# A fused decoder block on one core: first weights on ACT's queue, a 32-byte edge tile, projections in groups of six, and other queues at the seams

## The chip, the core and the metric

The kernel runs on one core of a Trainium2 chip. The core has five engines with in-order queues: TensorE (PE) multiplies matrices, VectorE (DVE), ScalarE (ACT) and GpSimd (POOL) do elementwise work, and SyncE (SP) mostly issues DMAs; ACT can issue DMAs too. The metric is the device time of one execution in microseconds; smaller is better. Every big product takes fp32 operands split in two parts (`ah`/`al`, `oh`/`ol`, `fh`/`fl`, `bh`/`bl`: a rounded high part, and the rest), so that one product of 128x128 by 128x512 costs three matmuls: high by high, high by low, low by high.

## What is computed

One decoder block on 1024 positions of 1024 channels, in float32:

```python
xn = rms_norm(x, norm1_g)
proj = xn @ w_in                      # 5632 columns
q_sb, k_sb, v_sb, q_hg, f_hg, i_hg, g_hg, gate_sb, gate_hg = split_cols(proj, IN_SIZES)
o_sb = stick_breaking_attention(rms_norm(heads(q_sb)), rms_norm(heads(k_sb)), heads(v_sb))
o_hg = hgrn2_mixer(q_hg, f_hg, i_hg, g_hg, lb, hg_norm_g)
mixed = sigmoid(gate_sb) * (o_sb @ w_branch[:512]) + sigmoid(gate_hg) * (o_hg @ w_branch[512:])
h = x + mixed @ w_out
hn = rms_norm(h, norm2_g)
out = h + (silu(hn @ w_gate) * (hn @ w_up)) @ w_down      # hidden size 2816
```

## The kernel before

`hybrid_block` is one program of six stages; the positions are handled in two halves of 512 columns (`hs(h)`).

**Start.** SP loads the small vectors (`vt`, L226) and then, in turn, pieces of x (`aa`) and the first four weight halves (`kb`). ACT loads its table at L205. Nine warm-up matmuls on `ones_r` run first. Each piece of x is scaled and split into `ah` (ACT) and `al` (DVE); each weight half into `oh` (POOL) and `ol` (DVE).

**Projections, attention and HGRN** (to about 701 us). All instructions of this stage are collected in a `Plan` and given out at L182 by a list scheduler: it walks a simulated clock and, on each engine, issues the ready instruction that comes first by rank and age. Ring buffers of fixed size (`pj` 3 banks, `z` 2, `ms` 3, `oh` and `ol` 4, `w` 2) hold work back. The projections (`proj`, moving operands `ah`/`al`, output `pj`) have the lowest rank and fill PE between the small products of attention and HGRN (`ms`, `z`). A projection is given out as eight pieces of three matmuls, one for each 128 rows of the contraction. `FILL` sets in which order the projected columns come. Finished heads are stored to `o_d`, gates before the sigmoid to `sig_d`.

**Mixing** (to about 790). SP loads the eight tiles `o_d` into `o32` (L785, ring `ld` of 4); ACT casts them to `oh` (L788), DVE subtracts for `ol` (L789). The branch weights `wb` are loaded through the ring `w` and split through the rings `oh`/`ol` of `wpool`. Gates `s0`, `s1` are loaded (L801, L802), multiplied by the row norm on POOL (L805), put through a sigmoid on ACT (L806), and multiplied into the products (L813, L814).

**wo** (to about 879). For each of eight 128-channel tiles and each half: SP loads a piece of x (`xx`, L856), PE multiplies, DVE adds (L859), SP stores h to `h_d` (L860), DVE scales by the second norm's gain (`yy`, L862), ACT squares and POOL sums the squares in `rr` (L870); DVE and ACT make the operands `fh`/`fl` of the next stage (`make`, L845, L846).

**Gate and up** (to about 1318). 11 rounds `p`, each with two 2x2 Winograd products of seven block products (`winograd`, `prod` at L916): 168 matmuls a round, moving operands `fh`/`fl`. In the first round, `begin` runs `channel_sums` (L924 to L931: the norm's sums over channels). Each round stores its result `c` (L1008) and four combinations `bs` (L1017) to `act_d`, on SP.

**Down** (to the end). Seven block products `o`, each a sum over 11 `p` into four banks `f` (L1060, L1062, L1064), moving operands `bh`/`bl` from `rb`, weights `ah`/`al` from `ra` (L1052, L1053, rings of 6 in `dB`). After the first product SP loads h into `hb` (L1069). After each product DVE adds the four banks to `hb` (L1077), and SP stores finished ones (L1079).

Tiles lie in pools; some are allocated from the right-hand end of a partition (`side="right"`): `rrp`, `qkp`, `const1`, `opool` (with mixing's `oh`, `ol`), `mt`, `s2p`, `fpool` (with `fh`, `fl`). In the program as built, tiles of the right-side pools start at byte addresses that are 32 modulo 64 (`fpool` from 106464, `opool` from 159712), tiles of the others at 0 modulo 64 (`xnp` and `mxp` from 26560, `dB` from 51136).

Of the kernel before, what the change touches and what calls it, by code (L numbers as in the profile page):

```python
# [10 lines left out]
F32 = mybir.dt.float32  # L11
# [4 lines left out]
ALU = mybir.AluOpType  # L16
# [3 lines left out]
P = 128  # L20
S = 1024
D = 1024
KT = D // P
HALF = 512
# [5 lines left out]
FILL = ["GgGGaifq", "gGaGfiqGG", "gaGGGiqGfGG", "gGGG"]  # L30
# [172 lines left out]
def hybrid_block(ctx: ExitStack, tc, xT, wi, wb, wo, wg, wu, wd, vec, outT):  # L203
    nc = tc.nc
    nc.scalar.preload_act_table_set("natural_log_exp_and_others")  # L205

# [19 lines left out]
    nc.sync.dma_start(vt, vec)  # L226
# [17 lines left out]

    rst = ExitStack()
# [47 lines left out]

    def hs(h):
        return slice(h * HALF, (h + 1) * HALF)
# [25 lines left out]
    xn = a_set(xst.enter_context(tc.tile_pool(name="xnp", bufs=1)))  # L321
    pre = ExitStack()
# [22 lines left out]
    st1 = ExitStack()  # L345
# [3 lines left out]
    hgp = st1.enter_context(tc.tile_pool(name="hgp", bufs=1, reuse_waits="tile"))  # L349
# [101 lines left out]
    def take_x(h):  # L451
        ss, acc, ws, sqs = new("ms"), new("tail"), [[], []], []
        for k in range(KT):
            x = new("aa" if h == 0 else ("xf", "xq", "xi", "xg")[k // 2])
            load(x, xT[k][:, hs(h)], 256)
            if h == 0 and k in (0, 1, 3, 4):
                u, i = k % 3, k // 3
                n, v = fill[u]
# [21 lines left out]
    def proj(ws, h, after=None):  # L480

        pss = [new("pj") for _ in ws]
        for k in range(KT):
            cols = slice(k % 4 * P, (k % 4 + 1) * P)
            for ps, w in zip(pss, ws):
                hi, lo = w[k // 4]
                last_fill[0] = M(1536, [
                    (ps, hi[:, cols], xh[k][h][:, hs(h)], k == 0, False),
                    (ps, hi[:, cols], xl[k][h][:, hs(h)], False, False),
                    (ps, lo[:, cols], xh[k][h][:, hs(h)], False, k == KT - 1)],  # L490
                    rank=-1, after=(last_fill[0], after))
            after = None
        return pss
# [67 lines left out]

    COL = {"q": 0, "k": 4, "v": 8, "hq": 12, "hf": 16, "hi": 20, "hg": 24, "G": 28}
# [182 lines left out]
    fill = [("q", 0), ("k", 0), ("v", 0), ("hf", 0), ("hq", 0), ("hi", 0)]  # L745
# [85 lines left out]
    with tc.tile_pool(name="wot", bufs=4, reuse_waits="tile") as ot_:  # L831
        seq = [0, 4, 1, 5, 2, 6, 3, 7]
        wq = [get_w(wo[seq.pop(0)])]
        for i in range(4):
# [14 lines left out]
            for e in range(2):  # L849
# [4 lines left out]
                for h in range(2):  # L854
# [5 lines left out]
                    nc.sync.dma_start(h_d[k][:, hs(h)], xx)  # L860
# [75 lines left out]
    with ExitStack() as sta:  # L936
# [24 lines left out]
        def winograd(a, c, begin=None):  # L961
# [3 lines left out]
            if begin:  # L965
                for ks in ((0, 1, 2), (3,)):
                    for o, bank in ((1, x), (5, z), (6, y)):
                        prod(bank, a[o], fop[o], True, ks)
                begin()
                nc.scalar.copy(p1, x)  # L970
# [8 lines left out]
            prod(x, a[2], fop[2], False)  # L979
# [9 lines left out]
        for p in range(NP):  # L989
# [18 lines left out]
            nc.sync.dma_start(act_d[p][:, :4 * HALF], c.rearrange("p b t -> p (b t)"))  # L1008
# [7 lines left out]
            for b, t in ((4, n7), (5, n6), (6, n5), (7, n4)):  # L1016
                nc.sync.dma_start(act_d[p][:, b * HALF:(b + 1) * HALF], t)  # L1017
# [15 lines left out]
          5: [(d + 4, 1) for d in range(4)], 3: [(d, 1) for d in range(4)]}  # L1033
    bank = [None] * 4
    for o in DOWN:
        first = o in (1, 6, 5)
        for p in range(NP):
            early = o == 1 and p < 4
            wp, tags = bp, btags = dB, ("ah", "al")
            btags = ("bh", "bl")  # L1040
            if early:

                rp = wpool if p < 2 else preB
                raw = rp.tile([P, 1024], F32, tag="w", bufs=2, name="w32")
                ra, rb = raw[:, :512], raw[:, 512:]
                if p < 3:
                    wp = bp = rp
                    tags = btags = ("oh", "ol") if p < 2 else ("ds", "ds")
            else:
                ra = dB.tile([P, HALF], F32, tag="ra", name="ra")  # L1050
                rb = dB.tile([P, HALF], F32, tag="rb", name="rb")
            nc.sync.dma_start(ra, LEFT[o](p))  # L1052
            nc.sync.dma_start(rb, blk(act_d[p], RIGHT[o]))  # L1053
            hi, lo = split(ra, wp, tags)
            bh, bl = split(rb, bp, btags)
            for d in range(4):
                if first and p == 0:
                    bank[d] = fb()
                ws = slice(d * P, (d + 1) * P)
                nc.tensor.matmul(bank[d], hi[:, ws], bh, start=first and p == 0, stop=False,  # L1060
                                 skip_group_check=True)
                nc.tensor.matmul(bank[d], hi[:, ws], bl, start=False, stop=False,  # L1062
                                 skip_group_check=True)
                nc.tensor.matmul(bank[d], lo[:, ws], bh, start=False, stop=p == NP - 1,  # L1064
                                 skip_group_check=True)
        if o == 1:
            for k, h in ([(d, 0) for d in range(4)] + [(d, 1) for d in range(8)]
                         + [(d, 0) for d in range(4, 8)]):
                nc.sync.dma_start(hb[k][:, hs(h)], h_d[k][:, hs(h)])  # L1069
            for d in range(4):  # L1070
                nc.scalar.copy(acc1[d], bank[d])
            continue
        for d, (k, h) in enumerate(TO[o]):
            t = hb[k][:, hs(h)]
            if o in (6, 7, 4):
                nc.vector.tensor_tensor(t, t, acc1[d], op=ALU.add)
            nc.vector.tensor_tensor(t, bank[d], t, op=ALU.add)  # L1077
# [50 lines left out]
```

## Time and profile before

| | us |
|---|---|
| median of 3 runs | 1542.43 (1540.65 to 1542.45) |
| the profiled execution | 1541.46 |
| its span | 1539.7 |
| PE busy | 1515.8 (98%) |
| DVE, ACT, POOL busy | 1184.3, 800.4, 178.8 |

Each page or view is of one profiled execution; times are microseconds from the start of the span. In rows of the timeline the columns are start, duration, engine, line, operation, output<-inputs, count, and in brackets the idle time of that engine just before and what ended it. In rows of groups the columns are line, engine, operation, output<-inputs, shapes, count, then total busy time and mean ns of one, then idle time before. Matmuls overlap in the pipeline, so the time that a matmul costs is the distance from one start to the next, not its own duration. `SPq` and `ACTq` rows are DMA issues on those queues.

The chain that ended last is shared out so: PE 73%, DVE 11%, DMA 6%, ACT 4%, of which `f L916` 25%, `pj L182` 23%, `ms L182` 8%, and `f` of the down stage 12%.

### The profile page before, as it was taken

What the parts mean: (1) busy time and instruction counts of PE and PEld (TensorE: products, weight loads), DVE (VectorE), ACT (ScalarE), POOL (GpSimd) and SP (SyncE); (2) the same over time, 40 slices, a digit from 0 to 9 for tenths busy, and PEclk for the clock granted to TensorE, in tenths of its full rate; (3) what the DMA queues carried; (4) which work ended last, traced back from release to release, by engine and by line L of the source; (5) the groups of instructions that cost most, each with busy time, mean ns of one, the idle gap of its engine ahead of it and who ended that gap; (6) DMA issues with size and microseconds to landing.
All of it is one profiled execution on the core that took longest, in us unless ns stands there. A gap on an engine that the chain in (4) does not pass through costs nothing.

```text
span 1539.7 us, 20478 instructions
## 1 busy us (share of the span) xinstructions
PE 1515.8 (98%) x7213; PEld 1242.1 (81%) x7213; DVE 1184.3 (77%) x2046; ACT 800.4 (52%) x1503; POOL 178.8 (12%) x202
## 2 busy tenths in 40 slices
PE   8999999999999999999999989999999999999999
PEld 6788888888888888888888868778778888778887
DVE  8899679988898768965567798888877777475553
ACT  7866778678768778454333352233333333254442
POOL 4211111111111101114412200000000000000000
PEclk9999999999999999999999999999999999999999
DMA  5111211111111121245334455666633332787672
GB/s 178 41 43 44 76 33 42 59 39 52 50 52 41 59 69 48 71 160 201 125 107 133 139 163 205 217 211 208 213 136 110 105 105 94 270 274 220 193 220 92
DMA packets 78407, 188.53 MB, mean 122 GB/s; under 512 B 9056, under 2 KB 11104, under 8 KB 76896
## 3 DMA queue, kind: packets, MB, share of 16 engines
q1 hardware_dynamic: 73696, 178.83, 35.5%
q10 hardware_dynamic: 4608, 8.39, 1.5%
q8 instruction: 57, 0.93, 0.3%
q14 instruction: 46, 0.38, 0.1%
HBM read 131.61 MB, written 55.57 MB: 122 GB/s over the span
## 4 chain that ended last, share of the span: by engine, by line
PE 73%; DVE 11%; DMA 6%; ACT 4%; issue 4%; POOL 1%; SPq 1%; DVEq 0%; POOLq 0%; ACTq 0%
PE f L916 25%; PE pj L182 23%; PE ms L182 8%; PE f L1062 4%; PE f L1064 4%; PE f L1060 4%; PE z L182 2%; DMA xx<-xT 2%; DVE ol L238 1%; ACT aa L182 1%; DMA rb<-act_d 1%; POOL s L805 1%; DMA s<-sig_d 1%; DVE aa L182 1%; DVE tail L182 1%
## 5 line engine op out<-in xcount | busy, mean ns | idle before, releaser
L182 PE MATMUL pj<-ah,oh 128*128 128x512 f32 x704 | 286.7, 407 | 2.0 <-POOL oh L182 2.0
L182 PE MATMUL pj<-ah,ol 128*128 128x512 f32 x704 | 277.3, 394 | 0.9 <-DVE ol L182 0.9
L182 PE MATMUL pj<-al,oh 128*128 128x512 f32 x704 | 276.0, 392 | 0.0
L916 PE MATMUL f<-fh,oh 128*128 128x512 f32 x616 | 244.0, 396 | 3.4 <-ACT p L970 1.7
L916 PE MATMUL f<-fl,oh 128*128 128x512 f32 x616 | 243.4, 395 | 0.7 <-DVE fl L846 0.7
L916 PE MATMUL f<-fh,ol 128*128 128x512 f32 x616 | 243.2, 395 | 0.6 <-DVE ol L238 0.6
L237 ACT CAST oh<-w 128x512 fp32r<-128x512 f32 x168 | 102.1, 620 | 175.2 <-PE f L916 137.9
L182 PEld LDWEIGHTS pj<-ah,ol 128*128 128x128 f32 x704 | 132.6, 188 | 31.6 <-DVE ol L182 2.1
L182 PEld LDWEIGHTS pj<-ah,oh 128*128 128x128 f32 x704 | 133.1, 189 | 25.3 <-POOL oh L182 2.9
L182 PEld LDWEIGHTS pj<-al,oh 128*128 128x128 f32 x704 | 133.2, 189 | 22.9 <-issue 0.5
L916 PEld LDWEIGHTS f<-fh,oh 128*128 128x128 f32 x616 | 115.4, 187 | 34.3 <-ACT p L970 2.1
L916 PEld LDWEIGHTS f<-fh,ol 128*128 128x128 f32 x616 | 115.4, 187 | 29.1 <-DVE ol L238 1.0
L916 PEld LDWEIGHTS f<-fl,oh 128*128 128x128 f32 x616 | 115.5, 187 | 29.0 <-DVE fl L846 1.0
L238 DVE TENSOR_TENSOR ol<-w,oh 128x512 fp32r<-128x512 f32 x168 | 114.7, 690 | 30.0 <-ACT oh L237 29.8
L1062 PE MATMUL f<-bl,ah 128*128 128x512 f32 x296 | 117.0, 395 | 1.3 <-DVE bl L238 1.3
L1060 PE MATMUL f<-bh,ah 128*128 128x512 f32 x296 | 114.6, 391 | 3.7 <-ACT bh L237 3.7
L182 DVE TENSOR_TENSOR_SCAN aa<-aa,ww 128x128 f32<-128x128 f32 (+3 forms) x96 | 92.3, 975 | 33.4 <-ACT aa L182 23.8
L182 POOL TENSOR_SCALAR oh<-w 128x512 fp32r<-128x512 f32 x84 | 70.9, 844 | 394.0 <-PE pj L182 348.6
L1064 PE MATMUL f<-bh,al 128*128 128x512 f32 x296 | 116.6, 394 | 0.0
L238 DVE TENSOR_TENSOR al<-ra,ah 128x512 fp32r<-128x512 f32 x73 | 50.4, 690 | 72.0 <-ACT ah L237 71.9
L237 ACT CAST ah<-ra 128x512 fp32r<-128x512 f32 x73 | 45.5, 623 | 101.8 <-PE f L1062 93.7
L182 ACT ACTIVATE aa<-aa 128x512 f32<-128x512 f32 (+3 forms) x128 | 69.1, 552 | 4.9 <-DVE aa L182 4.0
(273 smaller groups left out, 2996.7 us busy)
## 6 DMA issues: line engine op xcount, KB each, us to landing
w<-wi SPq DMA_DIRECT2D x42, 512.0 KB, 3.6
rb<-act_d SPq DMA_DIRECT2D x73, 256.0 KB, 4.1
w<-wg SPq DMA_DIRECT2D x22, 512.0 KB, 3.9
w<-wu SPq DMA_DIRECT2D x22, 512.0 KB, 4.1
w<-wd SPq DMA_DIRECT2D x22, 512.0 KB, 6.8
wd_d<-ds SPq DMA_DIRECT2D x44, 256.0 KB, 5.4
act_d<-c SPq DMA_DIRECT2D x11, 1024.0 KB, 3.9
act_d<-bs SPq DMA_DIRECT2D x44, 256.0 KB, 3.5
```

What stands on the lines that cost most here:

```text
L182: fn(*[a.real() if isinstance(a, View) else a for a in args], **{k: v.real() if isinstance(v, View) else v for k, v in kw.items()})
L237: pin(nc.scalar.copy(hi, src))
L238: pin(nc.vector.tensor_tensor(lo, src, hi.bitcast(F32), op=ALU.subtract))
L805: nc.gpsimd.tensor_tensor(s[:, hs(h)], s[:, hs(h)], rr1[h], op=ALU.mult)
L916: nc.tensor.matmul(out, a[i][:, ws], bl[k][j], start=start and k == 0 and i + j == 0, stop=k == 3 and i == 1, skip_group_check=True)
L1060: nc.tensor.matmul(bank[d], hi[:, ws], bh, start=first and p == 0, stop=False, skip_group_check=True)
L1062: nc.tensor.matmul(bank[d], hi[:, ws], bl, start=False, stop=False, skip_group_check=True)
L1064: nc.tensor.matmul(bank[d], lo[:, ws], bh, start=False, stop=p == NP - 1, skip_group_check=True)
```

## The change

1. The first weights (`first_w`) and `vt` are loaded on ACT's queue; ACT's table load comes behind them. The plan no longer counts these loads.
2. `proj` with one weight gives out six matmuls at a time (two pieces of the contraction), not three; the third entry of `FILL` is reordered.
3. An `edge` tile of 8 fp32 (32 bytes) is allocated first on the right-hand side and cleared once by POOL. All right-side tiles move down 32 bytes (`fpool` from 106432, `opool` from 159680): they start at 0 modulo 64. The pool `hgp` is opened earlier.
4. In wo, `h_d` is stored on ACT's queue, and DVE sums the squares.
5. In the first gate/up round the block products come in another order, and `p1` is copied before the channel sums.
6. The last round's `act_d` stores go on ACT's queue. `hb` is loaded on ACT's queue, two pieces after each `p` from 3 on of the first down product.
7. In the last down product the last three `p` are given out bank by bank, with each bank's add and store behind it.

```diff
-FILL = ["GgGGaifq", "gGaGfiqGG", "gaGGGiqGfGG", "gGGG"]
+FILL = ["GgGGaifq", "gGaGfiqGG", "gGaGGiqGfGG", "gGGG"]
...
-    nc.sync.dma_start(vt, vec)
+    nc.scalar.dma_start(vt, vec)
...
+    edge = ctx.enter_context(tc.tile_pool(name="edge", bufs=1, side="right"))
+    nc.gpsimd.memset(edge.tile([P, 8], F32, name="edge"), 0.0)
     rst = ExitStack()
     rrp = rst.enter_context(tc.tile_pool(name="rrp", bufs=1, side="right"))
...
+    first_w = []
+    for i in range(2):
+        for n, v in fill_cols[:2]:
+            t = hgp.tile([P, HALF], F32, tag="kb", bufs=4, name="kb")
+            nc.scalar.dma_start(t, wi[COL[n] + v][:, hs(i)])
+            first_w.append(t)
+    nc.scalar.preload_act_table_set("natural_log_exp_and_others")
...
-                w = new("kb")
-                load(w, wi[COL[n] + v][:, hs(i)], 256)
-                ws[u].append(split_w(w))
+                t = first_w[2 * i + u]
+                plan.ring("kb", 4)
+                ws[u].append(split_w(Buf("kb", lambda t=t: t)))
...
-        for k in range(KT):
-            cols = slice(k % 4 * P, (k % 4 + 1) * P)
+        step = 1 if len(ws) > 1 else 2
+        for k0 in range(0, KT, step):
             for ps, w in zip(pss, ws):
...
+                last_fill[0] = M(512 * len(mms), mms, rank=-1, after=(last_fill[0], after))
...
-                    nc.sync.dma_start(h_d[k][:, hs(h)], xx)
+                    nc.scalar.dma_start(h_d[k][:, hs(h)], xx)
...
-                        nc.gpsimd.tensor_tensor(rr[h], rr[h], sq, op=ALU.add)
+                        nc.vector.tensor_tensor(rr[h], rr[h], sq, op=ALU.add)
...
             if begin:
-                for ks in ((0, 1, 2), (3,)):
-                    for o, bank in ((1, x), (5, z), (6, y)):
-                        prod(bank, a[o], fop[o], True, ks)
+                prod(x, a[1], fop[1], True)
+                nc.scalar.copy(p1, x)
+                prod(z, a[5], fop[5], True)
+                prod(y, a[6], fop[6], True, range(3))
+                prod(x, a[2], fop[2], False)
+                prod(y, a[6], fop[6], True, (3,))
                 begin()
-                nc.scalar.copy(p1, x)
...
-            nc.sync.dma_start(act_d[p][:, :4 * HALF], c.rearrange("p b t -> p (b t)"))
+            store = nc.scalar.dma_start if p == NP - 1 else nc.sync.dma_start
+            store(act_d[p][:, :4 * HALF], c.rearrange("p b t -> p (b t)"))
...
+        for p in range(NP - LAST if final else NP):
+            ops = operands(o, p)
+            if o == 1 and p >= 3:
+                for k, h in HB[2 * p - 6:2 * p - 4]:
+                    nc.scalar.dma_start(hb[k][:, hs(h)], h_d[k][:, hs(h)])
...
+    rest = [(p, operands(o, p)) for p in range(NP - LAST, NP)]
+    for d in range(4):
+        for p, ops in rest:
+            step(d, p, ops, False)
+        finish(o, d)
```

Here `operands` loads and splits what one `p` needs, `step` issues the three matmuls of one bank, and `finish` adds a bank to `hb` and stores it: the bodies that stood in the loop before.

Three places in the order of instructions show what moves. The first is PE's queue where the projections end and mixing begins. Before, the last small product (`ms`) is followed by projections (`pj<-a...`) only, 129 of them; its first rows and the last three with the first of mixing (L302):

```order
L182 MATMUL ms<-th,ones_r 128x512
L182 MATMUL ms<-tl,ones_r 128x512
L182 MATMUL pj<-ah_161,oh 128x512
L182 MATMUL pj<-al_162,oh 128x512
L182 MATMUL pj<-ah_161,ol 128x512
...
L182 MATMUL pj<-ah_165,oh 128x512
L182 MATMUL pj<-al_166,oh 128x512
L182 MATMUL pj<-ah_165,ol 128x512
L302 MATMUL pj<-oh_7616,oh 128x512
```

With the change, the same place on PE, up to the first matmul of mixing (now L306):

```order
L182 MATMUL ms<-th,vv 128x128
L182 MATMUL ms<-tl,vv 128x128
L182 MATMUL pj<-ah_163,oh 128x512
L182 MATMUL pj<-al_164,oh 128x512
L182 MATMUL pj<-ah_163,ol 128x512
...
L182 MATMUL pj<-ah_169,oh 128x512
L182 MATMUL pj<-al_170,oh 128x512
L182 MATMUL pj<-ah_169,ol 128x512
L306 MATMUL pj<-oh_7621,oh 128x512 x2
```

Four groups of three, 12 projections, now follow the last small product, and the small products reach to just before mixing.

The second place is SP's queue at the same seam: `o<-o_d` are the loads of attention's output, `w<-wb` the branch weights, `s<-sig_d` the gates. Before:

```order
L230 DMA w_7682<-wb 128x1024
L182 DMA o_d_101<-tail 128x512
L785 DMA o_7614<-o_d_94 128x1024
L785 DMA o_7620<-o_d_95 128x1024
...
L785 DMA o_7656<-o_d_101 128x1024
L230 DMA w_7692<-wb 128x1024
L801 DMA s_7702<-sig_d_102 128x1024
```

With the change:

```order
L182 DMA o_d_101<-ot 64x256 x2
L228 DMA w_7869<-wb 128x1024
L796 DMA o_7619<-o_d_98 128x1024
L796 DMA o_7625<-o_d_99 128x1024
...
L796 DMA o_7661<-o_d_105 128x1024
L812 DMA s_7707<-sig_d_106 128x1024
L813 DMA s_7708<-sig_d_114 128x1024
```

Four loads of `wb` now stand ahead of the first `o` load. The fourth, `w_7869`, reuses a buffer whose split goes through the ring of four `oh`, and that ring's slot comes free with the last projection.

The third place is where gate/up ends and down begins. SP before (`act_d<-` are stores of the last round, `ra`/`rb` the operands of down, `hb` the reloads of h):

```order
L1069 DMA hb_12583<-h_d_141 128x512
L1008 DMA act_d_128<-c 128x2048
L1017 DMA act_d_128<-bs 128x512 x4
L1052 DMA ra<-wd 128x512
L1053 DMA rb<-act_d_122 128x512
...
L1053 DMA rb<-act_d_128 128x512
L1069 DMA hb_12584<-h_d_142 128x512
L1069 DMA hb_12585<-h_d_143 128x512
L1069 DMA hb_12582<-h_d_140 128x512
```

With the change these stores and reloads are on ACT, between its casts:

```order
L1095 DMA hb_12588<-h_d_145 128x512
L1023 DMA act_d_132<-c 128x2048
L1032 DMA act_d_132<-bs 128x512 x4
L235 CAST ah<-w_12672 128x512
L235 CAST bh<-w_12672 128x512
L1095 DMA hb_12589<-h_d_146 128x512
L235 CAST ah<-ra 128x512
L235 CAST bh<-rb 128x512
```

SP has only `ra` and `rb` loads there now, and ACT's casts for the fourth and later `p` stand behind the stores and, one pair each, behind reloads of `hb`.

More of the change, by code (lines that the diff above doesn't have):

```diff
@@ L1016, in hybrid_block @@
             for b, t in ((4, n7), (5, n6), (6, n5), (7, n4)):
[L1017 removed]
+                store(act_d[p][:, b * HALF:(b + 1) * HALF], t)
     fst.close()
@@ L1035, in hybrid_block @@
     for o in DOWN:
         first = o in (1, 6, 5)
[L1037 to L1055, printed above, removed]
+        final = o == DOWN[-1]
```

81 lines of the change are left out of this document (50 added, 31 removed).

## The prediction

> **What bounds the kernel now.** I read the page's first part, then the pitch of the big matmuls stage by stage from the windows, then the idle time of TensorE row by row. Windows give stretch, PE busy (x), PEld, DVE, ACT, POOL, granted clock, DMA share, GB/s.
>
> ```profile
> PE 1515.8 (98%) x7213; PEld 1242.1 (81%) x7213; DVE 1184.3 (77%) x2046; ACT 800.4 (52%) x1503; POOL 178.8 (12%) x202
> ...
> 710.00:750.00 40.00, 40.00 (x173) 32.11 (x172) 23.94 (x36) 14.65 (x21) 16.82 (x12) 1.00 0.41 138
> 800.00:870.00 70.00, 70.00 (x310) 57.98 (x309) 50.71 (x70) 25.46 (x44) 15.70 (x11) 1.00 0.43 139
> 1100.00:1300.00 200.00, 200.00 (x858) 160.51 (x858) 157.61 (x253) 63.46 (x106) 0.00 (x0) 1.00 0.35 117
> 1400.00:1500.00 100.00, 100.00 (x442) 82.81 (x442) 54.84 (x86) 42.02 (x74) 0.00 (x0) 1.00 0.67 204
> ```
>
> PE is busy for 98% of the span, so time can go in two ways only: a shorter pitch, or less of the idle time that PE has at the seams between stages. The pitch is not one number. Taking off the matmul cut at the edge, branch mixing (710) has 40/172 = 232.6 ns, the wo stage (800) 70/309 = 226.5, gate/up (1100) 200/857 = 233.4, and down (1400) 100/441 = 226.8 ns, all at full clock and without a gap. The slow stages are those whose moving operand lies in a right-side pool.
>
> **The change part by part.** The profiled execution took 1541.5 us (span 1539.7 and 1.8 around it), 1.0 under the median of 1542.4; I sum against 1541.5.
>
> *The edge tile.* It moves every right-side pool down by 32 bytes: moving operands in `opool` and `fpool` start at 32 modulo 64 bytes before and at 0 after. Left-side operands (`ah`/`al` of `xnp` and `mxp`, `bh`/`bl` of `dB`) are at 0 in both and are the ones read at 226.5 to 226.8. A row of 512 fp32 is 32 blocks of 64 bytes when aligned and 33 when shifted; 226.8 x 33/32 = 233.9, close to the 233.4 seen. So I take address as the cause.
>
> ```profile
> L916 PE MATMUL f<-fh,oh 128*128 128x512 f32 x616 | 244.0, 396 | 3.4 <-ACT p L970 1.7
> ...
> L302 PE MATMUL pj<-oh,oh 128*128 128x512 f32 x64 | 25.3, 395 | 0.0
> ```
>
> Gate/up has three such groups, 1848 matmuls x 6.6 ns = 12.2 us. Mixing has six groups of 62 to 64, 384 x 5.8 = 2.2. The 192 short score products that read `khl` get 0.3. **-14.7**, bounds 0 and -15. Against it: the slow operands also share a stage and the high end of a partition, and no row has an aligned mover up there, so place and address are not separated. Page of the Trainium skill "SBUF — State Buffer", Specifications, speaks against the gain: it gives 16-byte cachelines, by which a start at 32 is as good as one at 0 and this term is 0; no run here settles it, and the term above does not use it.
>
> *Start of the down stage (act_d stores to ACT, hb loads spread on ACT).*
>
> ```profile
> 1319.93 3.45 SPq L1017 DMA_DIRECT2D act_d<-bs  x4
> 1323.47 0.61 SPq L1052 DMA_DIRECT2D ra<-wd  x1
> ...
> 1330.58 1.50 PE L1060 MATMUL f<-bh,ah 128*128 128x512 f32 x4 [1.95 <-ACT bh L237]
> ...
> 1333.27 9.11 SPq L1069 DMA_DIRECT2D hb<-h_d  x14
> ...
> 1353.25 1.19 PE L1060 MATMUL f<-bh,ah 128*128 128x512 f32 x4 [1.71 <-ACT bh L237]
> 1355.72 0.80 PE L1062 MATMUL f<-bl,ah 128*128 128x512 f32 x1 [1.28 <-DVE bl L238]
> ...
> 1328.14:1337.22 9.08, 7.13 (x25) 5.41 (x24) 7.13 (x11) 6.68 (x11) 0.00 (x0) 0.81 1.02 376
> 1351.11:1362.51 11.40, 8.41 (x30) 6.21 (x30) 11.40 (x20) 9.13 (x18) 0.00 (x0) 0.85 0.79 265
> ```
>
> The `ra` loads sit on SP behind stores that wait for the last DVE products until 1323.47, so PE waits at 1330; then 14 `hb` loads take SP and the DMA for 9 us, the next product's operands come late, and PE waits at 1353. The first pause costs 9.08 - 23 x 0.2268 = 3.9, the second 11.28 - 28 x 0.2268 = 4.9, half clock (0.81 and 0.85) included. After, SP has no store ahead of its loads, and their buffers come free inside the last gate/up round. What is late next: ACT's casts for p = 3, which now stand behind the stores on ACT; the last `bs` leaves DVE before 1323.4; two casts of about 0.6 (half of the 1.06 of a 128x1024 cast below) and one 0.69 subtraction bring `bl` to 1325.3 or earlier, and PE needs it at 1317.7 + 3 x 2.72 = 1325.9. Sixteen `hb` loads on ACT's queue, two per 2.72 us, can hold a cast behind them while their transfers' slots are busy; the DMA is the nearest limit (0.5 + 0.5 MB per 2.72 us is 385 GB/s, and the first window shows 376 at a share of 1.02), but six operand pairs are loaded ahead. **-8.0**, bounds -3 and -8.8.
>
> *Seam between wo and gate/up (h_d stores to ACT, rr on DVE, first round reordered).*
>
> ```profile
> 878.64 0.32 SPq L860 DMA_DIRECT2D h_d<-xx  x1
> 879.05 0.38 SPq L856 DMA_DIRECT2D xx<-xT  x1
> ...
> 881.91 0.50 PE L916 MATMUL f<-fh,ol 128*128 128x512 f32 x1 [0.56 <-DVE ol L238]
> ...
> 882.94 0.69 DVE L859 TENSOR_TENSOR xx<-pj,xx 128x512 f32<-128x512 f32 x1 [1.09 <-DMA xx<-xT]
> ...
> 888.38 0.49 PE L916 MATMUL f<-fh,oh 128*128 128x512 f32 x1 [1.08 <-ACT fh L845]
> 889.53 0.50 PE L916 MATMUL f<-fl,oh 128*128 128x512 f32 x1 [0.66 <-DVE fl L846]
> 892.91 0.50 PE L916 MATMUL f<-fh,oh 128*128 128x512 f32 x1 [1.71 <-ACT p L970]
> 895.55 0.50 PE L916 MATMUL f<-fh,oh 128*128 128x512 f32 x1 [0.51 <-DVE g L971]
> ```
>
> The five pauses sum to 4.52 us, and with the refill after each this seam costs about 6. The chain is the last `xx` load, issued at 879.05 because a store that waits for DVE is ahead of it, landing at 882.9, then adds, casts, `fh` at 888. With stores gone from SP's queue the load leaves some us earlier; the last `fh` is wanted by matmul 45 instead of 33, and `p1` is copied while PE works on other banks. Left is one DVE add (0.69) between `a6` and `a7` behind the channel sums, about 0.3. The 14 to 16 `rr` adds moved from POOL to DVE cost about 15 x 0.69 = 10 us of a DVE that was busy 50.71 of 70 us in the wo window: hidden, 3 us at worst if DVE runs late there. **-4.5**, bounds -1.5 and -5.7.
>
> *Projections by six, and FILL.* Runs of projections between small products fall from 216 to 179.
>
> ```profile
> 664.41 2.73 PE pj L182 x12
> ...
> 668.93 3.44 PE pj L182 x15
> ...
> 672.83 29.27 PE pj L182 x129
> ...
> PE ms L182 <- DVE tl L182: 3.0, 4, 1.5
> PE z L182 <- DVE ww L182: 1.3, 3, 0.6
> PE ms L182 <- DVE kb L182: 1.2, 3, 0.5
> PE ms L182 <- ACT dl L182: 0.2, 1, 0.2
> ```
>
> A run of 15 takes 3.44 where 15 x 0.2268 is 3.40, and one of 12 takes 2.73 against 2.72: 0.01 to 0.04 lost per run, 37 x 0.024 = 0.9. PE's waits from 25 to 673 us sum to 5.7; the small products now come later against the projections, so I take 0.6 of that. **-1.5**, bounds -4 and +4.
>
> *What that adds behind it: a bare seam before mixing.* Before, 129 projections (29.27 us) follow the last small product; they cover the loading, casting and splitting of the attention outputs. After, 12 (2.7 us) follow it.
>
> ```profile
> 676.18 12.78 SPq L785 DMA_DIRECT2D o<-o_d  x8
> ...
> 681.41 3.06 ACT L788 CAST oh<-o 128x1024 fp32r<-128x1024 f32 x3 [0.45 <-ACT tmp L182]
> ...
> 694.72 1.06 ACT L788 CAST oh<-o 128x1024 fp32r<-128x1024 f32 x1 [1.63 <-DMA o<-o_d]
> ...
> 695.80 1.23 DVE L789 TENSOR_TENSOR ol<-o,oh 128x1024 fp32r<-128x1024 f32 x1 [1.46 <-ACT oh L788]
> ...
> 697.82 10.52 POOL L805 TENSOR_TENSOR s<-s,rr 128x512 f32<-128x512 f32 x8 [17.00 <-DMA s<-sig_d]
> ```
>
> From the first `o` issue to the last `ol` this took 697.0 - 676.2 = 20.9 us before, all under projections. After, the loads also stand on SP behind a `wb` load whose ring slot the last projection frees: with E its end, a weight's cast 0.6 and split 0.7 and the `wb` issue of 0.4 put the first `o` at about E + 1.9, its cast comes up to 5.2 us later (676.2 to 681.4 before), and PE starts at E + 7.5 to E + 8. `ol7` is done between E + 19 (one tile per 1.25 to 2 us) and E + 22.8. Then the gates: `s0` and `s1` load behind `o7`, POOL takes 4 x 1.3, ACT 1.06 each, so the first bank is free about E + 27.7. PE has by then been able to do 66 matmuls, 66 x 0.233 = 15.4 us. **+12**, bounds +5 (gates in time, `ol7` early) and +17. Page "TensorE: Matmul & The Clock Gate" of the Trainium skill, Part 1, puts PE at half clock for about 3.4 us after an idle window, which agrees with the 0.81 and 0.85 above; by it the first 66 matmuls would take 1.7 us more, here inside the waits.
>
> *Start (first weights on ACT's queue).*
>
> ```profile
> 5.99 0.74 PE L182 MATMUL pj<-al,oh 128*128 128x512 f32 x1
> ...
> 10.32 1.14 POOL L182 TENSOR_SCALAR oh<-kb 128x512 fp32r<-128x512 f32 x1 [1.15 <-DMA kb<-wi]
> ...
> 5.44:25.00 19.56, 16.62 (x57) 11.81 (x57) 18.09 (x27) 17.12 (x30) 5.39 (x9) 0.91 0.77 281
> ```
>
> Loads leave earlier, but DVE now has all four `ol` ahead of `al0`, so PE's second matmul waits for the fourth weight: that weight's cast was at 10.32, and comes up to 2 us earlier since it is issued earlier; plus 0.8 to 1.1 for the cast and twice about 0.7 on DVE (the 0.69 of such a subtraction), PE goes on at about 11.7 instead of 5.99. From there it runs without gaps, 1.7 us lost to half clock: by 25 us 52 matmuls against 57. **+1.5**, bounds -1 and +4.
>
> *Tail (last product bank by bank).*
>
> ```profile
> 1533.99 2.73 DVE L1077 TENSOR_TENSOR hb<-f,hb 128x512 f32<-128x512 f32 x4 [12.55 <-PE f L1064]
> ...
> 1535.60 0.39 PE L1064 MATMUL f<-bh,al 128*128 128x512 f32 x1
> ```
>
> Three of the four last adds and stores already end under the last matmuls' shadow; the last add, its store and landing stay, 4.1 us from 1535.60 to the span's end. Only crowding among the stores goes. **-0.5**, bounds 0 and -1.
>
> Sum: -14.7 - 8.0 - 4.5 - 1.5 - 0.5 + 12 + 1.5 = -15.7; 1541.5 - 15.7 = **1525.8 us**, or 1.0 more against the median of the runs shown, which I leave out as inside the measurement.
>
> **The rivals.** *Place, not address.* If the slow pitch comes from the high end of the partition or from the stage, the edge tile does nothing: 1525.8 + 14.7 = 1540.5. For: the confound above. Against: 33/32. The Trainium skill's page named above would give this time. *The seam is covered.* If loads of the early heads leave before the last projection and cover themselves, the +12 shrinks to nothing: 1513.8. For: `o_d0` is complete long before. Against: the order on SP. *Slower: the attention chain binds.* A ready small product waits on average half a group of projections: 0.34 us by three, 0.68 by six. If the chain of scores, scans and values is what sets the end of this stage, each of 179 visits comes 0.34 later, 61 us, 1587; it passes 1545.5 from 0.11 us per visit. For: DVE and ACT are busy there and mostly feed that chain. Against: PE waited 5.7 of 648 us, and 29 us of projections were left over.
>
> **How the numbers follow.** Forecast 0.64, seam covered 0.14, place 0.13, chain 0.09. Faster or slower counts from 0.2% (3.1 us), about what a measurement of this kernel can tell. The forecast's own bounds, with the large terms not all at one end, are 1515 to 1537; to hold 8 in 10 I go to 1512 and 1538, which leaves out the chain, most of place, and a strip below. Faster: 0.64 + 0.14 + 0.05 of place = 0.83; same 0.07; slower 0.08 of the chain and 0.02 of place = 0.10.
>
> **What would show it.** Right: gate/up at 226 to 227 ns a matmul; no PE wait on `bh` near the start of down; pauses under 1.5 us at the start of gate/up; a PE gap of 7 to 8 us where mixing begins, then gaps on `oh`, `ol` and a gate. Wrong: gate/up still at 233; no gap before mixing; more PE waits on `ww`, `tl` or `kb` in attention than 5.7; ACT's casts held by `hb` loads.

## The result and the profile after

The changed kernel took 1550.12 us (median of 4 runs, 1549.23 to 1550.82) against 1541.54 for the kernel before: ratio 1.0055, 95% interval 1.0038 to 1.0073. It is **slower by 0.55%**, where 1525.8 was forecast. The profiled span is 1548.8 us, 9.1 more than before.

The first table of the comparison is made from the starts of the matmuls in the two traces: from the first matmul of a stage to the first of the next (us). "Seam" is from the last projection to the first matmul of mixing. A half round of gate/up is 84 matmuls. "Gate/up, the rest" reaches to the first matmul of the down stage.

| stage | before | after | difference | forecast |
|---|---|---|---|---|
| to the 48th projection | 23.45 | 26.41 | +3.0 | +1.5 |
| on to the last projection | 678.26 | 678.77 | +0.5 | -1.5 |
| seam | 0.23 | 8.93 | +8.7 | with mixing |
| mixing | 89.60 | 94.85 | +5.3 | +12 - 2.3, seam and mixing together |
| wo | 87.08 | 87.04 | 0 | 0 |
| gate/up, first half round (84 matmuls) | 26.37 | 29.23 | +2.9 | -4.5 - 0.6 |
| gate/up, half rounds 1 to 10 | 196.93 | 197.53 | +0.6 | -5.6 |
| gate/up, the rest | 215.65 | 209.44 | -6.2 | -6.2 |
| down | 218.04 | 212.22 | -5.8 | -8.0 |
| last matmul to the end | 4.1 | 4.4 | +0.3 | -0.5 |

The forecasts of -0.6, -5.6, -6.2 and -2.3 are the edge tile's term, shared out to the stages. The pitch of the matmuls is read first, from the windows of the changed kernel (columns as in the prediction):

```profile
1100.00:1300.00 200.00, 199.32 (x879) 164.71 (x878) 163.15 (x263) 64.69 (x108) 0.00 (x0) 1.00 0.37 124
1400.00:1500.00 100.00, 100.00 (x443) 82.78 (x442) 54.50 (x86) 42.25 (x74) 0.00 (x0) 1.00 0.68 209
```

Gate/up now does 878 matmuls in 200 us where it did 857, and a half round without a wait takes 19.04 us instead of 19.60, 226.7 ns a matmul, the pitch of the down stage. But PE now waits: `PE busy` is 199.32, and the waits of PE from the start of gate/up on have new names. From the view of waits of the changed kernel (who waited for what: us in total, times, longest), 703 to 1332 us:

```profile
PE pj L306 <- ACT oh L799: 8.5, 1, 8.5
PE f L927 <- ACT p L978: 5.8, 1, 5.8
PE f L927 <- DVE g L989: 3.8, 5, 2.0
PE z L306 <- DVE t L825: 3.0, 4, 0.9
PE f L927 <- DVE g L994: 1.0, 1, 1.0
PE pj L306 <- DVE t L824: 0.7, 1, 0.7
```

In the kernel before, PE had no wait in this view between 905 and 1317 us. The timeline of the changed kernel at the seam before mixing:

```profile
714.11 1.22 PE L306 MATMUL pj<-oh,oh 128*128 128x512 f32 x2 [8.54 <-ACT oh L799]
...
713.01 1.04 ACT L799 CAST oh<-o 128x1024 fp32r<-128x1024 f32 x1 [6.53 <-DMA o<-o_d]
...
724.36 2.52 DVE L800 TENSOR_TENSOR ol<-o,oh 128x1024 fp32r<-128x1024 f32 x2
730.40 1.29 DVE L824 TENSOR_TENSOR t<-pj,s 128x512 f32<-128x512 f32 x2 [3.52 <-ACT s L817]
732.89 1.29 DVE L825 TENSOR_TENSOR t<-z,s 128x512 f32<-128x512 f32 x2 [1.21 <-ACT s L817]
...
707.17 12.34 SPq L796 DMA_DIRECT2D o<-o_d  x8
```

With the last projection ending near E = 705.4, the loads go out at E + 1.8, PE starts at E + 8.7, the last `ol` is done at E + 21.5, and the gate products start at E + 25.0 (`t<-pj,s`) and E + 27.5 (`t<-z,s`). The prediction's timetable had E + 1.9, E + 7.5 to 8, E + 19 to 22.8, and the first bank free at E + 27.7: the seam runs close to it, PE starting somewhat later and the first gate some 2 us earlier. At the seam before gate/up:

```profile
902.18 0.69 DVE L892 TENSOR_TENSOR t<-yy 128x512 f32<-128x512 f32 x1 [1.44 <-DMA h_d<-xx]
902.79 0.68 DVE L881 TENSOR_TENSOR rr<-rr,sq 128x512 f32<-128x512 f32 x1
903.39 0.68 DVE L893 TENSOR_TENSOR yy<-t,yy 128x512 f32<-128x512 f32 x1
...
907.01 0.68 DVE L897 TENSOR_TENSOR yy<-yy 128x512 f32<-128x512 f32 x1
...
907.73 0.62 ACT L856 CAST fh<-yy 128x512 fp32r<-128x512 f32 x1 [0.59 <-DVE yy L897]
908.25 0.61 ACT L235 CAST oh<-w 128x512 fp32r<-128x512 f32 x1
908.77 0.58 ACT L978 COPY p<-f 128x512 f32<-128x512 f32 x1
```

PE stops at 903.25 and goes on at 909.40. It wants to put `a2` in the bank that `p1` is copied from; the copy stands on ACT behind the casts of the last operands, and these wait for DVE, which works without a pause from 902.2 on, sums among its steps. In the down stage the operand loads are no longer late behind stores. On ACT's queue two reloads of h stand ahead of a cast:

```profile
1349.74 2.61 ACTq L1095 DMA_DIRECT2D hb<-h_d  x2
1352.39 0.62 ACT L235 CAST ah<-ra 128x512 fp32r<-128x512 f32 x1 [3.46 <-DMA rb<-act_d]
```

The two reloads take 2.6 us there, but the wait of the cast behind them is put down to the landing of `rb`. The down stage keeps some 2.9 us of short pauses between 1353 and 1366, in place of 8.8.

At the start the four first weights are issued at once, and share the DMA with x:

```profile
1.24 2.71 ACTq L333 DMA_DIRECT2D kb<-wi  x4
...
6.44 0.63 POOL L182 TENSOR_SCALAR oh<-kb 128x512 fp32r<-128x512 f32 x1 [2.61 <-DMA kb<-wi]
...
10.88 0.62 POOL L182 TENSOR_SCALAR oh<-kb 128x512 fp32r<-128x512 f32 x1 [0.70 <-DMA kb<-wi]
...
11.54 0.69 DVE L182 TENSOR_TENSOR ol<-kb,oh 128x512 fp32r<-128x512 f32 x1 [0.62 <-POOL oh L182]
12.15 0.75 DVE L182 SCALAR_TENSOR_TENSOR al<-aa,vt,ah 128x512 fp32r<-128x512 f32 x1
...
12.95 0.79 PE L182 MATMUL pj<-al,oh 128*128 128x512 f32 x1 [5.33 <-DVE al L182]
```

PE's second matmul is at 12.95 instead of 5.99: `al` stands behind all four `ol` on DVE. The fourth weight's cast, at 10.88 here, was this one before:

```profile
11.68 0.81 POOL L182 TENSOR_SCALAR oh<-kb 128x512 fp32r<-128x512 f32 x1 [0.22 <-DMA kb<-wi]
```

### The profile page after: what moved, and what is told of

Same layout as the page of the kernel before. It is cut to its first block, busy times and chain, and to the rows that moved or that the text cites. A ratio compares the mean times of both kernels' runs of the same rounds, so it can differ in the third digit from the quotient of the medians.

```text
span 1548.8 us, 20470 instructions
## 1 busy us (share of the span) xinstructions
PE 1505.8 (97%) x7213; PEld 1245.1 (80%) x7213; DVE 1187.2 (77%) x2060; ACT 801.4 (52%) x1503; POOL 156.1 (10%) x189
## 4 chain that ended last, share of the span: by engine, by line
PE 49%; DVE 9%; DMA 6%; issue 3%; ACT 2%; POOL 1%; POOLq 0%; SPq 0%; ACTq 0%; DVEq 0%
PE f L927 19%; PE f L1076 12%; PE pj L182 8%; PE ms L182 3%; PE pj L306 2%; PE pj L307 2%; PE pj L308 2%; DVE ol L236 1%; DMA w<-wu 1%; DMA s<-sig_d 1%; DMA rb<-act_d 1%; POOL s L816 1%; PE z L182 1%; DMA h_d<-xx 1%; DVE bs L1024 1%
## 5 line engine op out<-in xcount | busy, mean ns | idle before, releaser
L182 DVE TENSOR_TENSOR_SCAN aa<-aa,ww 128x512 f32<-128x512 f32 (+3 forms) x96 | 94.0, 995 | 26.3 <-ACT ww L182 15.3
L182 POOL TENSOR_SCALAR oh<-w 128x512 fp32r<-128x512 f32 x84 | 66.5, 791 | 436.1 <-PE pj L182 324.6
```

Of the source, the lines that this page charges most:

```text
L182: fn(*[a.real() if isinstance(a, View) else a for a in args], **{k: v.real() if isinstance(v, View) else v for k, v in kw.items()})
```

## The experiments

Each time is a median, with its ratio to the kernel before on the same chip and the 95% interval. "Seam + mixing" is from the last projection to the first matmul of wo; it is 89.8 before and 103.8 after. "First half" is gate/up's first half round. The columns by stage are from the one profiled execution of each run, which differs from the median by up to 5 us (in e8 it is 4.9 us under it, in e10 4.6 over it).

| run | us | ratio, interval | seam + mixing | first half | half rounds 1 to 10 | down |
|---|---|---|---|---|---|---|
| e1 | 1532.68 | 0.9949 (0.9928 to 0.9969) | 88.5 | 26.19 | 195.54 | 218.06 |
| e2 | 1555.74 | 1.0097 (1.0077 to 1.0116) | 104.2 | 29.24 | 197.92 | 212.10 |
| e3 | 1547.10 | 1.0041 (1.0028 to 1.0054) | 104.1 | 29.00 | 194.96 | 211.55 |
| e4 | 1543.92 | 1.0029 (1.0016 to 1.0041) | 103.8 | 26.01 | 194.48 | 212.08 |
| e5 | 1554.85 | 1.0090 (1.0071 to 1.0110) | 106.0 | 30.01 | 197.52 | 211.75 |
| e6 | 1557.66 | 1.0106 (1.0089 to 1.0124) | 104.6 | 30.18 | 198.77 | 212.23 |
| e7 | 1545.30 | 1.0027 (1.0017 to 1.0037) | 103.6 | 29.86 | 194.43 | 211.69 |
| e8 | 1544.04 | 1.0020 (1.0007 to 1.0032) | 103.3 | 26.07 | 194.41 | 211.34 |
| e9 | 1545.31 | 1.0029 (1.0018 to 1.0041) | 100.7 | 29.05 | 195.23 | 211.92 |
| e10 | 1524.72 | 0.9900 (0.9883 to 0.9918) | 87.5 | 26.00 | 196.13 | 213.62 |
| e11 | 1529.31 | 0.9922 (0.9905 to 0.9939) | 88.4 | 25.95 | 195.70 | 214.41 |
| e12 | 1561.81 | 1.0135 (1.0116 to 1.0154) | 87.4 | 29.92 | 225.39 | 213.29 |
| e13 | 1526.83 | 0.9907 (0.9888 to 0.9925) | 88.6 | 26.44 | 197.31 | 211.65 |
| e14 | 1529.76 | 0.9927 (0.9910 to 0.9944) | 89.0 | 26.09 | 196.08 | 213.51 |
| e15 | 1533.61 | 0.9959 (0.9944 to 0.9973) | 94.3 | 29.66 | 194.07 | 211.55 |
| e16 | 1555.42 | 1.0093 (1.0077 to 1.0109) | 102.8 | 26.09 | 198.15 | 219.39 |

**e1 and e2: is the pitch set by the address?** e1 is the kernel before with the edge tile, e2 the changed kernel without it.

```diff
     # e1
+    edge = ctx.enter_context(tc.tile_pool(name="edge", bufs=1, side="right"))
+    nc.gpsimd.memset(edge.tile([P, 8], F32, name="edge"), 0.0)
     rst = ExitStack()
```

> The kernel before plus the edge tile alone. Address theory: a gate/up matmul costs 226.8 ns instead of 233.3 (half rounds of 19.05 us instead of 19.60) and mixing loses 2 us, so the time falls by 11 to 15 us to 1527 to 1531; if DVE cannot follow the faster PE, a few us of it come back as PE waits on g and c in gate/up. Rival (the place in the partition, or the stage, sets the slow pitch): no change, 1541 to 1543.

> The changed kernel without the edge tile. Address theory: half rounds of gate/up go back to 19.60 us and the time rises from 1550 by 8 to 14 us (less than the full 14.5 if the waits on DVE in gate/up, 5 to 6 us, come only from the faster PE). Rival: stays at 1549 to 1551.

The same window of e1 and then of e2 (shifted with the stage by 10 us), and e1's waits in gate/up from 903 to 1309 us:

```profile
1100.00:1300.00 200.00, 199.40 (x880) 164.76 (x879) 158.35 (x253) 64.83 (x109) 0.00 (x0) 1.00 0.34 116
```

```profile
1110.00:1310.00 200.00, 199.96 (x857) 160.37 (x856) 155.46 (x248) 62.24 (x103) 0.00 (x0) 1.00 0.36 122
```

```profile
PE f L918 <- DVE g L978: 4.5, 5, 1.4
```

The address decides: 32 bytes alone bring 857 matmuls to 879 in the same window, at the same place high in the partition and in the same stage, so the rival "place" falls. But the whole run becomes 8.2 us shorter, not 14.7: seam and mixing by 1.3 and gate/up by 6.8. In the first rounds DVE now comes late with `g`, and PE waits 4.5 us in all. Four of these five waits fall ahead of the window above, where DVE is busy for 158 of 200 us: they fall where DVE has more to do. The window of 1000 to 1100 us, before and in e1:

```profile
1000.00:1100.00 100.00, 99.92 (x427) 79.64 (x426) 88.50 (x144) 30.61 (x51) 0.00 (x0) 1.00 0.65 222
1000.00:1100.00 100.00, 97.09 (x427) 79.41 (x426) 88.64 (x145) 30.46 (x52) 0.00 (x0) 1.00 0.65 221
```

DVE is busy for 88.5 us of 100 there. Its 44 operations of `down_sums`, of 0.684 us each, all lie between 896 and 1111 us in the kernel before, that is in the first rounds. e1 has them there too, and from 1138 us on each of its half rounds takes 19.04 us. e2 takes 5.6 us more than the changed kernel: without the edge tile, the rest of gate/up is 6.2 us longer, while half rounds 1 to 10 take nearly as long as with it (197.92 against 197.53). e2's forecast of 8 to 14 was too high.

**e3 and e4: what stops PE at the start of gate/up?** e3 puts the first round back in the old order, e4 puts the sums back on POOL.

```diff
     # e4
-                        nc.vector.tensor_tensor(rr[h], rr[h], sq, op=ALU.add)
+                        nc.gpsimd.tensor_tensor(rr[h], rr[h], sq, op=ALU.add)
```

> The changed kernel with the first gate/up round in the order of before. Theory: PE's 5.9 us wait at the start of gate/up is made by a2 being put ahead of the last a6 piece: a2 writes the bank that p1 is copied from, and that copy stands on ACT behind casts of the last operands; with the old order the first half round takes 24 to 26 us instead of 29.2 and the time is 1545 to 1547. Rival (DVE is late with the last operands, whatever the order on PE): the wait only moves to fh or fl, first half round 28 to 29 us, time 1549 to 1551.

> The changed kernel with the squares summed on POOL again. Theory that the p1 copy sets the wait: the wait at the start of gate/up shrinks by at most 1.5 us, the waits on g in the following rounds stay, 1548 to 1550. Rival (DVE's added 10 us of sums make it late at the seam and in the first rounds): the first half round falls by 3 us and the waits on g by 3 to 5, 1542 to 1545.

My theory fell. With the old order (e3) the wait on `p1` shrinks from 5.8 to 1.1, and a wait on DVE's operands of the channel sums (`parts`) has its place; PE's waits there:

```profile
PE f L940 <- DVE parts L936: 3.3, 1, 3.3
PE f L927 <- ACT fh L856: 1.2, 1, 1.2
PE f L927 <- ACT p L981: 1.1, 1, 1.1
```

With the sums on POOL and the new order (e4):

```profile
PE f L927 <- ACT fh L856: 1.3, 1, 1.3
PE f L927 <- ACT p L978: 1.3, 1, 1.3
```

The half round takes 29.0 in e3 and 26.0 in e4. The sums on DVE cost 3.2 us there (29.23 - 26.01); the copy was only where the delay came out. The other runs agree: with the sums on DVE the first half round takes 29.00 to 30.18 us, with the sums on POOL 25.95 to 26.44 (e12 apart, whose other edit loads POOL).

Half rounds 1 to 10 take 3.0 us less in e4 too, but that the sums make this is not shown: e3, e7, e9 and e15 keep them on DVE and take 194.1 to 195.2. Most of the difference is one half round of 22.99 us in the changed kernel, 20.19 in e4. In it PE waits 2.0 us for `g`, the longest of the five such waits shown above, and some eight matmuls behind it come 0.43 us apart instead of 0.23. e5 and e6 have such a half round as well, e13 too with the sums on POOL (22.93), and e3, e7, e9 and e15 have none; why is open.

**e5, e6, e7: what makes the seam before mixing?** One part of the plan undone each: three matmuls at a time, the old `FILL`, the old start.

```diff
     # e5
-        step = 1 if len(ws) > 1 else 2
+        step = 1
     # e6
-FILL = ["GgGGaifq", "gGaGfiqGG", "gGaGGiqGfGG", "gGGG"]
+FILL = ["GgGGaifq", "gGaGfiqGG", "gaGGGiqGfGG", "gGGG"]
```

> The changed kernel with projections given out three at a time. 97 projections then follow the last small product instead of 12 (22 us against 2.7). Theory (groups of six make attention's small products later against the projections, and the cover of mixing's loads is used up): the gap before mixing falls from 8.9 to under 1 us, mixing from 94.9 to 87.5 to 88.5, the time to 1533 to 1537. Rival (the order of FILL or the new start makes the seam): gap stays, 1546 to 1550.

> The changed kernel with FILL's third entry of before, still six at a time: 18 projections follow the last small product. Theory: gap before mixing 7 to 8.5 us, time 1547 to 1550. Rival (FILL makes the seam): gap under 2, 1534 to 1538.

> The changed kernel with vt and the first weights loaded by SP inside the plan again. If the second matmul's wait for all four weights costs the start 1 to 3 us, the 48th projection is back at 23.5 us. 54 projections (12 us) then follow the last small product, so by the cover theory the gap before mixing is 0 to 3 us and mixing 89 to 92: time 1537 to 1542. Rival (cover does not decide; only the start changes): 1547 to 1549.

e5 contradicts the prediction's reason as the whole cause: with 96 projections (22 us; its expectation counts 97) behind the last small product the gap is still 8.1 us. e7, with 54, has 7.9, and e6, with 18 and the old `FILL`, has 9.0. The start's cost shows in e7: the 48th projection is at 23.85 instead of 26.41, the last one 2.7 us earlier. That cost is not the same in every execution: the 48th projection comes at 24.30 to 26.54 us in the seven profiles with the new start, and at 23.15 to 23.95 in those with the old one. e5 and e6 also end the projections later, at 710.7 and 707.7 instead of 705.2; I don't know why, except that the list scheduler gives out another order.

**e8, e9, e10: cover, or place.** e8 has the old plan whole (start, groups of three, `FILL`), so 129 projections behind the last small product, and the sums on POOL.

> The start, the groups of three, FILL and the sums on POOL as before; the edge tile, the stores of h on ACT, the new order of the first gate/up round, and the down stage's queues and last product as in the change. If the parts add up: 1532.7 (the kernel before with the edge tile alone) less 6 us in the down stage, gate/up's first half round 25.5 to 26.2: 1525 to 1528. Rival (the first round's new order stalls on p1's copy even without the sums on DVE): first half round 28 to 29, 1529 to 1531.

The seam stayed, at 8.4 us; the first half round was right. The wait in e8, with the old order of work on PE:

```profile
PE pj L307 <- ACT oh L793: 8.0, 1, 8.0
```

SP's queue in e8, with one `wb` load before these three:

```profile
680.78 22.04 SPq L229 DMA_DIRECT2D w<-wb  x3
702.91 11.79 SPq L790 DMA_DIRECT2D o<-o_d  x8
```

What e8 still had of the change was the pool `hgp`, opened ahead of `tmpp`, `stk` and `att`. In the programs as built, `tmpp`'s two buffers move from 92096 and 94144 to 133632 and 135680. Mixing's second load buffer lies at 131008 to 135104, over the first of them, and its `s0` over the second. In the changed kernel the last gate lies in the first of them: the second `o` load must wait for that gate's store out of `tmp`, which the last projection fills. In e8 (and in e16 below) the last gate lies in the second, under `s0`, and it is the gate before it whose store the `o` load needs; that store is issued at 696.5 in e8. But four `wb` loads stand ahead of all `o` loads on SP, in the changed kernel as in e8, and the `o` loads leave only when the last of them has gone. I take it that the scheduler puts them there because the overlap makes the `o` load late; that step is not shown by itself. What the runs can show is what the order of the pools does. In e9 (the changed kernel) and e10 (e8) the pools are opened in the old order:

```diff
+    tmpp = st1.enter_context(tc.tile_pool(name="tmpp", bufs=1, reuse_waits="tile"))
+    stk = st1.enter_context(tc.tile_pool(name="stk", bufs=1, reuse_waits="tile"))
+    att = st1.enter_context(tc.tile_pool(name="att", bufs=1, reuse_waits="tile"))
     hgp = st1.enter_context(tc.tile_pool(name="hgp", bufs=1, reuse_waits="tile"))
```

> The changed kernel with the pools tmpp, stk and att opened ahead of hgp, so that all four lie at the addresses of before. Theory (the seam before mixing comes from place: in the changed kernel mixing's load buffer at 131008 lies over the buffer tmp at 133632, which the last gate's store empties): gap before mixing under 2 us instead of 8.9, mixing 88 to 91 instead of 94.9, time 1533 to 1538. Rival, the prediction's own theory (only 12 projections cover the loads): gap 6 to 9, 1546 to 1550. Both at work: gap 3 to 5.

> The kernel with start, groups of three, FILL and sums on POOL as before, edge tile and the rest as in the change (which kept a gap of 8.4 us before mixing with 129 projections after the last small product), with the pool order of before. Place theory: gap 0.2, mixing 87.5 to 88.5, time 1524 to 1528. Rival (something else in that kernel holds the loads): gap stays at 8, 1540 to 1544.

In e10 the `o` loads leave at 676.8 us, as early as in the kernel before (676.2). Its seam and mixing take 87.5 us, 15.7 less than e8's. But e9's still take 100.7: a gap of 4.1, and gates that come late. There the `o` loads stand behind the last store of attention's output on SP, in the timeline of e9:

```profile
695.77 8.89 SPq L182 DMA_DIRECT2D o_d<-ot  x2
704.71 11.97 SPq L796 DMA_DIRECT2D o<-o_d  x8
```

With 12 projections behind the last small product, that store is made just before the end. So both causes are real, and each is nearly enough alone: the pool order (place) 15.7 (e8 against e10), short cover 13.2 (e9 against e10), both together 16.2 (the changed kernel against e10). Short cover stands here for the three edits that make it, the start, the groups of six and `FILL`.

**e15 and e16: each cause by itself.** e15 is the changed kernel with the old start and the old pool order, e16 the kernel before with `hgp` opened first and nothing else.

> The changed kernel with the old start and with the pool order of before: 54 projections (12 us) follow the last small product, and no buffer of mixing lies over tmp. Cover theory: gap and mixing together between 87.5 (129 projections, e10) and 100.7 (12, e9): 90 to 94. Rival (with 54 it is as with 12, since loads of o wait for something else): 99 to 101.

> The kernel before with only one edit: hgp opened ahead of tmpp, stk and att, as the change does. Place theory: same order of projections and small products as before, but the loads of o wait for the last gate's store: gap 8 to 9 us, gap and mixing 103 to 106 instead of 89.8, time 1554 to 1558. Rival (place is harmless without the rest): 1540 to 1543.

e16 makes the seam out of nothing else: its wait, and the time 1555.4, 14.9 above the kernel before, 13.0 of it in seam and mixing.

```profile
PE pj L302 <- ACT oh L788: 7.8, 1, 7.8
```

In e15, without a gap, seam and mixing take 94.3, between 87.5 (129 projections) and 100.7 (12): cover counts too, about 6.4 us between 12 and 54 (e9 against e15, which differ in the start).

**e11 and e14: the reloads of h.** e11 puts them on SP, one after each p of the first two down products; e14 does so on ACT.

```diff
-            if o == 1 and p >= 3:
-                for k, h in HB[2 * p - 6:2 * p - 4]:
-                    nc.scalar.dma_start(hb[k][:, hs(h)], h_d[k][:, hs(h)])
+            if (o == 1 and p >= 3) or (o == 2 and p < 8):
+                k, h = HB[p - 3 if o == 1 else p + 8]
+                nc.sync.dma_start(hb[k][:, hs(h)], h_d[k][:, hs(h)])
```

> As the kernel before it, with the reloads of h on SP, one piece after each p of the first two down products, instead of two on ACT. If ACT's casts are held by those reloads (2.4 us of pauses in the down stage): down 209.5 to 210.5 us instead of 211.3 to 212.2, time 1 to 2 us lower. Rival (on SP they hold the operand loads, as before): down 214 or more.

> e10 with the reloads of h on ACT one after each p of the first two down products instead of two after each p of the first. If the reloads hold ACT's casts: down 210 to 211.5 us instead of 213.6. Rival (the operand loads are late whatever ACT does): 212.5 to 214.

Neither helps: down is 214.4 and 213.5 us, and 211.3 to 213.6 in the runs with the change's way. What holds the last 2 to 4 us of that stage is open.

**e12: relieve DVE in gate/up.** The four subtractions and additions of `down_sums` go to POOL, which is idle there.

> As the kernel before it, with the four combinations of w_down (ds) made on POOL. If DVE's backlog makes the waits on g in the first rounds of gate/up (about 5 us): half rounds 1 to 10 together 190.5 to 192 instead of 194.4, time 2.5 to 4 us lower. Rival (DVE and POOL slow each other, or the order and not the load sets the waits): no change or slower.

A miss: half rounds 1 to 10 take 225.4 instead of 195.7 (e11). From the groups of 930 to 1000 us, e12 first, then e10:

```profile
L947 POOL TENSOR_TENSOR ds<-w,ds 128x512 f32<-128x512 f32 x10 | 16.7, 1672 | 11.3 <-DMA w<-wd 9.8 <-issue 1.3
L237 DVE TENSOR_TENSOR ol<-w,oh 128x512 fp32r<-128x512 f32 x17 | 14.9, 892 | 6.0 <-ACT oh L236 6.0
L907 DVE TENSOR_TENSOR w<-s,w 128x512 f32<-128x512 f32 x3 | 4.5, 1502 | 0.1
```

```profile
L237 DVE TENSOR_TENSOR ol<-w,oh 128x512 fp32r<-128x512 f32 x20 | 13.5, 684 | 1.3 <-ACT oh L236 1.2
L907 DVE TENSOR_TENSOR w<-s,w 128x512 f32<-128x512 f32 x4 | 2.7, 687 | 0.1
```

Beside POOL the same DVE subtraction takes 892 or 1502 ns instead of 684 or 687, and POOL's own takes 1672.

**e13: what the rest of the gate/up seam is worth.** e10 with h stored on SP and the first round in the old order.

> e10 with the stores of h on SP and the first gate/up round in the order of before, so that of the change only the edge tile and the down stage's edits are left. If stores and order give nothing (DVE's chain sets that seam): first half round 26.0 to 26.4 us, time within 1.5 us of e10. Rival (the prediction's: they free the last load of x and hide p1's copy): first half round 29 or more, 3 to 5 us slower than e10.

26.44 us against 26.00: stores and order are worth 0.4. e10 and e13 beat both kernels, 1.0% and 0.9% under the kernel before; they cannot be told apart. What both keep of the change is the edge tile and the down stage's edits.

## Why the prediction was wrong

The forecast of the span was 1524.0 and it came to 1548.8. The 24.8 us between them are shared out by the prediction's own steps: gate/up 6.2, its seam 7.9, the seam before mixing 4.2, start and projections 3.5, down 2.2, tail 0.8.

- *The edge tile, -14.7.* The mechanism was right and so was the size of the pitch: 22 half rounds x 0.56 = 12.3 us in gate/up. The step that failed is the silence behind it: whether DVE would follow a PE that is 3% faster was not asked. The prediction's window shows DVE at 157.61 of 200 us, and there it does follow; in the first rounds it was at 88.50 of 100, and there 6.2 us came back as waits on DVE (half rounds 1 to 10: 197.53, where ten of 19.04 are 190.4, against 196.93 and ten of 19.60 before). e1 shows such waits with the edge tile alone (195.54). The rule that a start at 32 is as good as one at 0, which the prediction took from the 16-byte cachelines of the Trainium skill's page "SBUF — State Buffer", Specifications, is refuted for these reads by e1.
- *Seam wo to gate/up, -4.5, was +3.4 (2.86 and the 0.56 of pitch): 7.9 us, the largest error, and of the wrong sign.* The failed sentence is that the sums on DVE are "hidden, 3 us at worst". They cost 3.2 (e4). I measured DVE's slack over the wo stage and not in its last microseconds, where one engine makes the last operands and all else queues behind it. The gains that I counted beside it, the freed load of x and the hidden copy, are worth 0.4 (e13). The load of x was freed, but another wait came in its place: DVE waited 1.09 us for the last `xx` before, and in e10 and the changed kernel it waits 1.84 and 1.44 for a store of h (`h_d<-xx`, at L892 above) to land, since `t7` takes the buffer of an earlier `xx`. That this wait is why so little was gained is likely, not shown by itself.
- *Seam before mixing, +12, was +16.2: 4.2 us.* Right in place and timetable, wrong in cause by half. The short cover is worth 13.2 by itself, so the size of the term was about right for its own reason; the pool order is worth 15.7 by itself, in a move that the prediction does not mention. The timetable was close because it was read from SP's queue as it is, with the `wb` load ahead of the `o` loads. But that `wb` load comes with the pool order and not with the short cover: e8 and e16 have it with 129 projections as cover, e9 and e10 issue it behind the `o` loads. The late gates were in the sum; four further waits on them (`z <- t`, 3.0) were not.
- *Start +1.5 and projections -1.5 were +3.0 and +0.5.* PE went on at 12.95 where 11.7 was reckoned. The prediction misread a row: 10.32 is the cast of the third weight, and the fourth's was at 11.68. It came 0.8 us earlier (10.88), not up to 2 earlier than 10.32, and the first weight's came later (6.44 instead of 4.72). All of them and x share the DMA engines, which are full there (a share of 1.03 to 1.06 from 6 to 12 us). Fewer runs of projections gained nothing (678.1 in e15, with six at a time, against 677.8 in e13, with three).
- *Down -8.0 was -5.8.* Stores and operand loads did what was said; short pauses of 2.9 us stayed. The reason given for a loss there, casts held behind reloads on ACT, was not confirmed: e14 halves the reloads' pace without a gain. What makes these pauses stays open.
- *Tail -0.5 was +0.3*, within what runs differ by.
- *The rivals.* "Place, not address" fell by e1. "Covered seam" fell: the seam was bare. "The attention chain binds" fell too: that stage kept its length (+0.5). The range went wrong because each cost was bounded on its own: the seam before mixing and the start came near their bad bounds together, the seam to gate/up (+3.4) left its bounds (-1.5 to -5.7), and the give-back in gate/up had none.

## What to carry to other kernels

When a change makes the engine that bounds a stage faster, look in the same stage for the engine next to it in load, in short windows and not over the whole stage, and price what it gives back; and put nothing on the engine that makes the last operands before a seam. When a change moves where a pool is opened, compare the addresses of the next stage's first buffers with the last buffers of the stage before: opening one pool earlier cost 13 to 16 us here (e16, e8), and no line of the diff names the overlap of 1.5 KB that came with it. Moving an operand's start from 32 to 0 modulo 64 bytes made its matmuls 3% cheaper here, for 32 bytes of memory.

## What the hardware showed

The moving operand of 128x512 fp32r costs 233.3 ns a matmul from a start of 32 modulo 64 bytes and 226.7 from 0 (e1, e2). The ratio, 1.029, is near 33/32; that blocks of 64 bytes are the reason is not shown. DVE subtractions of two SBUF operands slow from 684 to 892 ns and more beside POOL ones, and POOL's from 1293 (median of its `s` products before) to 1672 (e12); the Trainium skill's page "SBUF — State Buffer", section "SBUF: two separate sides", says that the two share a port pair that one of them holds for a whole instruction, which fits this direction.
